# Two operands of an embedding land in pages of the weights' ring, and an empty job stands ahead of the output matrix's last two rows

## The chip, the cores and the metric

The kernel runs on one core of a Trainium2 chip. A core has five engines that matter here, each with a queue of its own that it works off in order: TensorE (PE in the profile; its weight loads are PEld), VectorE (DVE), ScalarE (ACT), GpSimd (POOL) and SyncE (SP), which here only issues DMA transfers. The metric is the device time of one execution in microseconds (us), the median of several runs.

## The reference

The reference is an encoder of two layers over 1024 tokens of width 1024, all in float32. Layer 0 mixes tokens by neighbourhood attention (16 heads of 64, a window of 8 by 16 tokens on a 16 x 64 grid, a learned bias by offset); layer 1 by dense differential attention (8 heads, two softmaxes each). After the mixer each layer has a gated ConvGLU of inner width 2816 and then a gated embedding of the layer's own input `p`:

```python
for i in range(DEPTH):
    h = rms_norm(x, g[0])
    m = neighborhood_attention(...) if i % 2 == 0 else diff_attention(...)
    x = x + rms_norm(m, g[1])
    f = conv_glu_ffn(rms_norm(x, g[2]), ...)
    x = x + rms_norm(f, g[3])
    gate = sigmoid(rms_norm(x, g[4]) @ ple_w_gate[i])
    x = x + gate * (p[i] @ ple_w_proj[i])
```

Two products of this concern the change: `p[i] @ ple_w_proj[i]` (1024 x 256 by 256 x 1024), which depends on no token mixer and so can be computed early, and the attention's own output product with `na_w_o` (`da_w_o` in layer 1), 1024 x 1024.

## The kernel before, in words

**Float32 by three products.** Every operand of a matmul is split into a high part (a rounding copy on ACT, `high`, L135) and a low part (the difference, on DVE, `low`, L138); `mm3` (L172 to L174) multiplies high by high, high by low and low by high. So a page of 128 x 1024 that comes from memory costs one ACT instruction and one DVE instruction before PE can use it.

**Pools.** `raw` has three pages and takes what DMA loads; `ws` has four pages, the ring of the weights: each block of the projection's weights takes two (high and low), and later the embedding's results `e` and the strips of the attention's output take them too. `r1` and `r2` have four pages of 128 x 4096 each; `r1` holds the normed input of the layer, `r2` the queries, keys and values of two pairs of heads. A page is taken again when all who read it are done. All pages of a pool have one size, 4 KB a partition in `raw` and in `ws`.

**The stream.** In `na` (L528) a loop over 64 units (16 heads by 4 pairs of column blocks) computes for unit n+1 the scores and the softmax (`na_scores`), turns unit n's weights (`na_turn`, two groups) and multiplies unit n-2 with its values (`na_values`). In between `tick` draws steps from a generator, `qkv_stream` (L296), so that the projection of the next pair of heads fills PE. At the last pair (j = 7) the stream has four more things at its end: after the first half of the last value projection (L383) it begins `embeddings` (L440), which brings in two blocks of rows of `pT` and two of `ple_w_proj`, splits the four into the pages `a` and `b` of `r2`, and later multiplies them, 8 blocks of tokens by 2 halves, into pages `e` that are written to `pp` (L1476 to L1484); it calls `last_rows` (L707); and it runs `first_out` (L790), the part of the output product that needs only the first seven pairs' results. In layer 0 `embeddings` calls `load_split` four times, each with a page of `raw`; in layer 1 the four are loaded and split one at a time by jobs.

**Jobs.** `last_rows` issues loads of the eight rows of blocks of the output matrix and leaves nine jobs in a list: split rows 0 to 5, then `part` (split the first strip of the attention's output, loaded in row 4's job; it also issues row 7's load), then rows 6 and 7 (row 6's load is issued by row 5's job). One job is drawn at the end of `na_scores` (L471) and one at the end of the second `na_turn` (L492), and its ACT and DVE instructions are ordered behind that step's own on the same engine. In layer 1 `da_scores` (L617) and `da_turn` (L633) draw them in the same way: `last_rows` is shared by both layers. `row` and `first_out` draw jobs themselves where something that they need is not there yet.

**The second strip.** `mix_out` (L803) begins after the loop. Its first act is `second = self.out_part(...)` (L829): a strip of the attention's output is loaded into a page of `raw` and split into two pages of `ws`.

**Order.** PE's instructions stand in the order in which the program is written (L1550). Those of ACT, DVE, POOL and SP are ordered by a planner when the program is built: it takes what is ready by its own account of time, earlier lines of the program first. A wait then holds all that stands behind it in that engine's queue.

Of the kernel before, what the change touches and what calls it, by code (L numbers as in the profile page):

```python
# [91 lines left out]
class Trunk:  # L92
# [27 lines left out]
    def page(self, pool, tag, shape=(P, D), dt=F32, **k):  # L120
        return pool.tile(list(shape), dt, tag=tag, name=self.uid(tag), **k)
# [84 lines left out]
    def bcast(self, pool, tag, row, **k):  # L206
        t = self.page(pool, tag, **k)
        self.nc.sync.dma_start(t, row.partition_broadcast(P))
        return t
# [497 lines left out]
    def last_rows(self, layer):  # L707


        nc = self.nc  # L710
        src = self.i[("na_w_o", "da_w_o")[layer]]
        self.W, self.part0 = [], None
        page = lambda dt=F32R: self.page(self.r1, "r1", (P, 4, D), dt)
        pages = [page(), page(), page(F32)]
        raw = {}

        def load(kt):
            if kt < 4:
                raw[kt] = pages[2][:, kt]
            else:  # L720
                raw[kt] = self.page(self.raw, "raw")
            nc.sync.dma_start(raw[kt], src[kt * P : kt * P + P])

        def row(kt):
            if kt == 4:
                del pages[2]
                pages.extend([page(), page()])
            hi, lo = pages[2 * (kt // 4) : 2 * (kt // 4) + 2]
            parts = hi[:, kt % 4], lo[:, kt % 4]
            did = self.split(raw.pop(kt), *parts)  # L730
            self.W.append(parts)
            if kt == 4:
                raw["part"] = self.part_raw(layer, 0)
            if kt == 5:
                load(6)
            return did

        def part():
            self.part0 = self.part_of(raw.pop("part"))
            load(7)  # L740
            return self.did

        for kt in range(6):
            load(kt)
        self.jobs += [lambda kt=kt: row(kt) for kt in range(6)] + [part] + [lambda kt=kt: row(kt) for kt in (6, 7)]

    def job(self, act, dve):

        if self.jobs:
            self.behind(self.jobs.pop(0)(), (act, dve))  # L750

    def row(self, kt):

        while len(self.W) <= kt:
            self.jobs.pop(0)()
        return self.W[kt]

    def times(self, out, sta, mov, first=True):
# [31 lines left out]
    def first_out(self):  # L790

        while self.part0 is None:
            self.jobs.pop(0)()
        hi, lo = self.part0
        m = [self.bank(self.pj), self.bank(self.pj)]
        yield
        yield from self.times_steps(
            m, [(hi[:, k], lo[:, k]) for k in range(KT - 1)], (self.row(k) for k in range(KT - 1)), last=False
        )
        self.row(KT - 1)  # L800
        self.out0 = hi, lo, m
# [638 lines left out]
    def embeddings(self, layer):  # L1440

        nc = self.nc
        a = self.page(self.r2, "r2", (P, 2, 2, SEQ), F32R)
        b = self.page(self.r2, "r2", (P, 2, 2, D), F32R)
        load = []
        for k in range(2):
            rows = slice(k * P, k * P + P)
            for o, src in ((a, self.i["pT"]), (b, self.i["ple_w_proj"])):
                load.append((src[layer][rows], o[:, k, 0], o[:, k, 1]))
        if layer == 0:  # L1450
            for src, *parts in load:
                self.load_split(src, dst=parts)
        else:
            left = list(load)

            def begin(src, *parts):
                raw = self.page(self.raw, "raw")
                nc.sync.dma_start(raw, src)
                return raw, parts

            next_one = [begin(*left.pop(0))]

            def job():
                raw, parts = next_one.pop()
                did = self.split(raw, *parts)
                if left:
                    next_one.append(begin(*left.pop(0)))
                return did

            self.jobs += [job] * 4  # L1470
        yield
        while layer == 1 and next_one:
            self.jobs.pop(0)()
        for t in range(NT):
            s = slice(t * P, t * P + P)
            e = self.page(self.ws, "ws")  # L1476
            for half in range(2):
                w = slice(half * 512, half * 512 + 512)
                o = self.bank(self.pj)
                for k in range(2):  # L1480
                    self.mm3(o, (a[:, k, 0, s], a[:, k, 1, s]), (b[:, k, 0, w], b[:, k, 1, w]), k == 0, k == 1)
                    yield
                nc.scalar.activation(e[:, w], o, AF.Copy)  # L1483
            nc.sync.dma_start(self.pp[layer][s], e)  # L1484
# [127 lines left out]
```

## Time and profile before

| | |
|---|---|
| Median of 3 runs | 2758.91 us (2757.64 to 2758.96) |
| Profiled execution | 2758.85 us, of which the span from first to last instruction is 2757.1 us |
| Mean granted TensorE clock | 0.993 |
| PE busy | 2693.7 us, 98% of the span |
| PEld, DVE, ACT, POOL busy | 81%, 70%, 48%, 17% |
| DMA in the two stages' ends | the last 60 us of neighbourhood attention are 430 to 490 us; those of differential attention 1850 to 1930 us |

PE's share of busy time is a mean over all stages; what happens at one place is read from the waits, the timeline and the granted clock of that place. The granted clock is 1.00 or 0.50 in stretches of 3.4 us or a multiple of it. "SPq" rows are DMA issues: their time is that of the issue, and the wait for the landing shows in the instruction that needs the data.

### The profile page before, as it was taken

To read this page: it belongs to the slowest core of one execution; us is meant where nothing else is said; L and a number is where in the kernel's file an instruction comes from. 1 tells how busy PE (TensorE), PEld (TensorE's weight loads), DVE (VectorE), ACT (ScalarE), POOL (GpSimd) and SP (SyncE) were. 2 spreads that over 40 slices of the span, in tenths; PEclk is the share of its full clock that TensorE was granted. 3 is DMA by queue.
4 is the path that set the end of the run, shared out by engine and by line. 5 is a ranking of instruction groups with operands and counts; after the bars stand their busy time and mean duration, and the time that the engine had idled before them with its cause. 6 is when DMAs were issued, how large, how long until landed. Compare 5 with 4: busy or idle time off the path is not lost.

```text
span 2757.1 us, 36537 instructions
## 1 busy us (share of the span) xinstructions
PE 2693.7 (98%) x13440; PEld 2225.7 (81%) x13440; DVE 1938.5 (70%) x3317; ACT 1321.2 (48%) x2467; POOL 463.2 (17%) x461
## 2 busy tenths in 40 slices
PE   7999998999999999999999999999999999999998
PEld 5788887877888888888788888887887888888887
DVE  5677776579777777676566666676688777776664
ACT  4555556454444445454355555555454434444452
POOL 2121220004333310001000000000105333300000
PEclk9999999999999999999999999999999999999999
DMA  6512214533322373343211111123413323272342
GB/s 183 169 55 68 66 48 156 142 92 107 115 102 94 115 263 125 105 150 111 99 46 46 45 46 46 53 77 126 134 62 122 115 92 115 98 284 96 115 146 103
DMA packets 129476, 298.48 MB, mean 108 GB/s; under 512 B 11753, under 2 KB 37737, under 8 KB 129297
## 3 DMA queue, kind: packets, MB, share of 16 engines
q1 hardware_dynamic: 129296, 296.15, 32.5%
q8 instruction: 105, 1.72, 0.3%
q14 instruction: 75, 0.61, 0.1%
HBM read 221.69 MB, written 86.61 MB: 112 GB/s over the span
## 4 chain that ended last, share of the span: by engine, by line
PE 85%; DVE 6%; DMA 4%; ACT 2%; issue 2%; POOL 0%; SPq 0%; ACTq 0%; POOLq 0%; DVEq 0%
PE b L172 19%; PE b L173 19%; PE b L174 19%; PE g L770 6%; PE m L770 5%; PE b L642 4%; PE s L606 3%; PE b L628 2%; PE b L203 2%; PE av L512 1%; PE b L485 1%; DVE r L138 1%; PE b L770 1%; DMA raw<-in_qkv 1%; DMA x<-in_x 1%
## 5 line engine op out<-in xcount | busy, mean ns | idle before, releaser
L172 PE MATMUL b<-r,ws 128*128 128x512 f32 (+1 forms) x1328 | 547.3, 412 | 6.9 <-ACT ws L135 3.7
L173 PE MATMUL b<-r,ws 128*128 128x512 f32 (+1 forms) x1328 | 519.7, 391 | 1.4 <-DVE r L138 1.2
L174 PE MATMUL b<-r,ws 128*128 128x512 f32 (+1 forms) x1328 | 519.1, 391 | 0.5 <-DVE ws L138 0.5
L172 PEld LDWEIGHTS b<-r,ws 128*128 128x128 f32 x1328 | 252.8, 190 | 55.2 <-ACT ws L135 4.1
L174 PEld LDWEIGHTS b<-r,ws 128*128 128x128 f32 x1328 | 252.1, 190 | 54.8 <-DVE ws L138 1.0
L173 PEld LDWEIGHTS b<-r,ws 128*128 128x128 f32 x1328 | 253.3, 191 | 38.6 <-DVE r L138 3.5
L172 PE MATMUL b<-r,r 128*128 128x512 f32 x680 | 270.4, 398 | 9.5 <-ACT r L135 5.2
L184 POOL TENSOR_TENSOR ss<-ss,mhalf 128x1 f32<-128x1 f32 x136 | 84.0, 619 | 1142.1 <-DVE ss L646 563.3
L172 PE MATMUL b<-r,wa 128*128 128x512 f32 x688 | 269.0, 391 | 4.5 <-DVE B L1140 3.7
L445 ACT ACTIVATE E<-E,mn 128x1024 f32<-128x1024 f32 (+2 forms) x256 | 221.4, 866 | 105.2 <-DVE mn L441 104.7
L174 PE MATMUL b<-r,wa 128*128 128x512 f32 x688 | 268.6, 390 | 0.0
L173 PE MATMUL b<-r,wa 128*128 128x512 f32 x688 | 268.4, 390 | 0.0
L174 PE MATMUL b<-r,r 128*128 128x512 f32 x680 | 266.5, 392 | 1.0 <-DVE r L138 1.0
L173 PE MATMUL b<-r,r 128*128 128x512 f32 x680 | 266.8, 392 | 0.5 <-DVE r L138 0.5
L138 DVE TENSOR_TENSOR ws<-raw,ws 128x512 fp32r<-128x512 f32 (+3 forms) x168 | 171.1, 1026 | 61.1 <-ACT ws L135 58.6
L138 DVE TENSOR_TENSOR r<-raw,r 128x512 fp32r<-128x512 f32 (+1 forms) x170 | 129.1, 766 | 113.1 <-ACT r L135 110.0
L135 ACT ACTIVATE r<-raw 128x512 fp32r<-128x512 f32 (+1 forms) x170 | 112.7, 670 | 193.2 <-PE b L173 162.6
L135 ACT ACTIVATE ws<-raw 128x512 fp32r<-128x512 f32 (+3 forms) x168 | 124.3, 748 | 137.4 <-PE b L174 52.1
L172 PEld LDWEIGHTS b<-r,r 128*128 128x128 f32 x680 | 128.6, 189 | 38.6 <-ACT ws L1483 6.3
L770 PE MATMUL m<-r,ws 128*128 128x512 f32 x672 | 156.9, 393 | 0.0
L172 PEld LDWEIGHTS b<-r,wa 128*128 128x128 f32 x688 | 129.4, 188 | 33.5 <-DVE B L1140 5.2
L770 PE MATMUL g<-r,ws 128*128 128x512 f32 x672 | 155.8, 391 | 0.0
(178 smaller groups left out, 5110.4 us busy)
## 6 DMA issues: line engine op xcount, KB each, us to landing
raw<-in_w_in SPq DMA_DIRECT2D x86, 512.0 KB, 3.5
raw<-in_qkv SPq DMA_DIRECT2D x48, 512.0 KB, 5.6
spillS<-r SPq DMA_DIRECT2D x88, 256.0 KB, 3.2
r<-in_ffn_w_out SPq DMA_DIRECT2D x40, 512.0 KB, 10.1
raw<-spillS SPq DMA_DIRECT2D x40, 512.0 KB, 3.5
spillA<-B SPq DMA_DIRECT2D x66, 256.0 KB, 2.9
raw<-spillA SPq DMA_DIRECT2D x30, 512.0 KB, 4.0
x<-x SPq DMA_DIRECT2D x24, 512.0 KB, 3.7
```

What stands on the lines that cost most here:

```text
L135: return self.nc.scalar.activation(hi, src, AF.Copy).ins
L138: return self.nc.vector.tensor_tensor(out=lo, in0=src, in1=hi.bitcast(F32), op=ALU.subtract).ins
L172: mm(out, sta[0], mov[0], start=first, stop=False, skip_group_check=onto)
L173: mm(out, sta[0], mov[1], start=False, stop=False, skip_group_check=onto)
L174: mm(out, sta[1], mov[0], start=False, stop=last, skip_group_check=onto)
L184: self.nc.gpsimd.tensor_tensor(out=ss, in0=ss, in1=self.mhalf, op=ALU.pow)
L203: self.nc.tensor.transpose(t[:, k * P : k * P + P], h[:, c : c + P], self.ident)
L445: self.exp = nc.scalar.activation(e, e, AF.Exp, bias=mn, scale=-1.0, accum_out=sm).ins
L606: nc.tensor.matmul(s[m][:, w], A[o, a, q], A[o, b, w], start=z == 0, stop=z == 2)
L628: nc.tensor.transpose(t[:, k * P : k * P + P], w[:, c : c + P], self.ident)
L642: nc.tensor.matmul(o, wT[:, k], V[:, k], start=k == 0, stop=k == KT - 1)
L770: mm(out[half], a, b[:, w], start=first and k + z == 0, stop=last and k == n - 1 and z == 2)
```

## The change

There are two edits. In layer 0's `embeddings` the four pages into which DMA loads are taken first, in the order `raw`, `ws`, `ws`, `raw`, and then each operand is loaded and split: the second and the third (the first block of `ple_w_proj`, the second of `pT`) land in pages of `ws`. In `last_rows` the list of jobs gets an entry `None` after `part`: the step that draws it has nothing to add, and rows 6 and 7 are drawn one step later, in both layers. The places that draw a job are taught to skip an empty one (`hurry`, and a test in `job`).

```diff
-        self.jobs += [lambda kt=kt: row(kt) for kt in range(6)] + [part] + [lambda kt=kt: row(kt) for kt in (6, 7)]
+        self.jobs += [lambda kt=kt: row(kt) for kt in range(6)] + [part, None] + [lambda kt=kt: row(kt) for kt in (6, 7)]

     def job(self, act, dve):

         if self.jobs:
-            self.behind(self.jobs.pop(0)(), (act, dve))
+            todo = self.jobs.pop(0)
+            if todo:
+                self.behind(todo(), (act, dve))
+
+    def hurry(self):
+
+        todo = self.jobs.pop(0)
+        if todo:
+            todo()

     def row(self, kt):

         while len(self.W) <= kt:
-            self.jobs.pop(0)()
+            self.hurry()
         return self.W[kt]
...
         if layer == 0:
-            for src, *parts in load:
-                self.load_split(src, dst=parts)
+            raws = [self.page(p, t) for p, t in ((self.raw, "raw"), (self.ws, "ws"), (self.ws, "ws"), (self.raw, "raw"))]
+            for raw, (src, *parts) in zip(raws, load):
+                nc.sync.dma_start(raw, src)
+                self.split(raw, *parts)
```

`first_out` and the wait loop of layer 1's `embeddings` call `hurry` in the same way.

More of the change, by code (lines that the diff above doesn't have):

```diff
@@ L792, in first_out @@
         while self.part0 is None:
-            self.jobs.pop(0)()
+            self.hurry()
         hi, lo = self.part0
@@ L1472, in embeddings @@
         while layer == 1 and next_one:
-            self.jobs.pop(0)()
+            self.hurry()
         for t in range(NT):
```

## The prediction

> **What bounds the kernel now.** I read the page first, for the span and the chain that ended last; then PE's waits around the end of neighbourhood attention; then that stretch by windows, with the granted clock; then the timelines of SP, ACT and DVE there.
>
> ```profile
> span 2757.1 us, 36537 instructions
> PE 85%; DVE 6%; DMA 4%; ACT 2%; issue 2%; POOL 0%; SPq 0%; ACTq 0%; POOLq 0%; DVEq 0%
> ```
>
> PE sets the time nearly everywhere; a gain can come only where PE waits, or from the clock that it is granted behind a wait. In 430 to 500 us, the end of neighbourhood attention, these are PE's longest waits (total, times, longest):
>
> ```profile
> PE b L172 <- ACT r L135: 5.2, 1, 5.2
> PE b L172 <- ACT ws L1483: 3.3, 1, 3.3
> PE b L770 <- ACT ws L1483: 1.3, 1, 1.3
> ```
>
> Windows of that stretch (length; busy time and count of PE, PEld, DVE, ACT, POOL; granted clock; DMA share, GB/s) show that the two long waits each cost twice: PE is then granted half of its clock for 6.8 us.
>
> ```profile
> 433.30:440.10 6.80, 1.79 (x11) 1.25 (x9) 3.44 (x7) 3.04 (x7) 0.00 (x0) 1.00 0.98 360
> 440.10:447.00 6.90, 5.71 (x15) 4.32 (x16) 3.44 (x10) 3.45 (x8) 0.00 (x0) 0.51 0.25 85
> 470.80:477.70 6.90, 6.25 (x17) 5.29 (x18) 3.00 (x9) 3.30 (x9) 0.00 (x0) 0.51 0.57 178
> ```
>
> The chain that ended last names what the waits hang on (start, length): a load of the embedding for the first, a row of the output matrix for the second, a store of `pp` for the third.
>
> ```profile
> 431.90 7.79 DMA raw<-in_ple_w_proj
> 464.26 5.57 DMA raw<-in_na_w_o
> 478.80 3.09 DMA pp<-ws
> ```
>
> **The change, part by part. First, the embedding's operands.** No instruction is added: four loads, four ACT copies and four DVE differences stay. Only the pages, and so the times of the loads, move. SP's issues before:
>
> ```profile
> 390.42 0.38 SPq L161 DMA_DIRECT2D raw<-in_pT  x1
> 402.38 0.33 SPq L161 DMA_DIRECT2D raw<-in_ple_w_proj  x1
> 427.50 1.75 SPq L722 DMA_DIRECT2D r<-in_na_w_o  x4
> 429.37 0.60 SPq L161 DMA_DIRECT2D raw<-in_pT  x1
> ```
>
> The first two take the free pages of `raw`; the last two wait until the first two are split, and then queue behind four rows of the output matrix: the fourth lands 7.79 us after 431.90. In the changed kernel the fourth operand takes the page of 402.38, and the second and third need two pages of `ws`. The last weights of queries leave theirs when PE has read them, at 415:
>
> ```profile
> 414.94 0.39 PE L174 MATMUL b<-r,ws 128*128 128x512 f32 x1
> 415.20:426.50 11.30, 11.30 (x63) 9.75 (x62) 7.29 (x22) 6.28 (x16) 0.00 (x0) 1.00 0.01 1
> ```
>
> There DMA is idle (share 0.01), and SP issues nothing between 402.38 and 427.50, so nobody stands behind these two as they wait for PE. Even at the jam's 7.79 us they land by 423, before the first split could run:
>
> ```profile
> 426.52 1.05 ACT L135 ACTIVATE r<-raw 128x1024 fp32r<-128x1024 f32 x1
> 434.77 0.60 ACT L135 ACTIVATE r<-b 128x512 fp32r<-128x512 f32 x1 [0.47 <-PE b L203]
> 439.71 1.06 ACT L135 ACTIVATE r<-raw 128x1024 fp32r<-128x1024 f32 x1 [1.49 <-DMA raw<-in_ple_w_proj]
> 440.80 1.23 DVE L138 TENSOR_TENSOR r<-raw,r 128x1024 fp32r<-128x1024 f32 x1 [1.32 <-ACT r L135]
> 442.08 0.79 PE L173 MATMUL b<-r,r 128*128 128x512 f32 x1 [0.47 <-DVE r L138]
> 427.60:435.40 7.80, 7.14 (x42) 5.84 (x40) 6.56 (x14) 5.28 (x11) 0.00 (x0) 1.00 0.89 288
> ```
>
> The late splits then move from the stall (439.71 on ACT is the later) in among the work of the last unit but five. That cover is thin: from 427.6 to 435.4 DVE is busy 6.56 of 7.80 us, and two more differences are 2 x 1.23 = 2.46, so 6.56 + 2.46 - 7.80 = 1.2 us do not fit and reach PE through the softmax and the evacuations. If instead the planner leaves both splits where they stand now, behind the last evacuation of values (ACT free at 435.3), they end at about 435.3 + 1.05 + 1.23 + 1.23 = 438.8. PE's two waits of 5.2 + 0.47 = 5.7 us so shrink by 5.7 - 1.2 = 4.5 at best and by 442.1 - 438.8 = 3.3 at worst. I take 4.2, near the best, because the planner takes earlier lines first and the splits' lines are early.
>
> The clock: 5.71 us of PE at 0.51 did the work of 2.9, so 2.8 us were lost. Smaller waits can cost a stretch too:
>
> ```profile
> 638.10:641.50 3.40, 1.22 (x6) 0.77 (x5) 3.40 (x5) 1.95 (x4) 2.10 (x2) 1.00 0.52 190
> 641.50:644.90 3.40, 3.40 (x10) 2.62 (x9) 3.40 (x6) 0.00 (x0) 0.86 (x2) 0.50 0.67 211
> ```
>
> Here PE was busy 1.22 of 3.4 us (its one wait is 2.18) and got half the clock for the next 3.4: 1.7 us. With a wait of 1.4 to 2 PE is busy over 40% of such a stretch and I take no loss; the bound is 1.7. **First term: 4.2 + 2.8 = 7.0 us; bounds 3.3 + 1.1 = 4.4, and 5.7 + 2.8 = 8.5.**
>
> [...]
>
> **Second, the empty job in layer 0.**
>
> ```profile
> 467.38 0.84 ACT L135 ACTIVATE Ahi<-b 128x512 fp32r<-128x512 f32 x2
> 469.85 1.06 ACT L135 ACTIVATE r<-raw 128x1024 fp32r<-128x1024 f32 x1 [1.63 <-DMA raw<-in_na_w_o]
> 470.82 1.06 ACT L1483 ACTIVATE ws<-b 128x512 f32<-128x512 f32 x2
> ```
>
> Row 6's copy waits 1.63 us for its load and runs 1.0; behind it stand two evacuations that PE waits for. One step later (behind the next exponentials) its load, landed at 469.83, is there. The evacuation then starts at 468.2 instead of 470.82, and PE's wait of 3.3 falls to about 0.6: 2.7 us. The clock stretch after it goes: 6.25 us at 0.51, 3.1 us. Row 7 moves from where row 6 then stands to behind the following turn; its load, issued when the first strip is split, has some 6 us, against 5.57 for row 6's.
>
> What is late next is the second strip, whose load takes the page that row 6 leaves:
>
> ```profile
> 472.33 0.38 SPq L779 DMA_DIRECT2D raw<-oT  x1
> 477.19 1.05 ACT L135 ACTIVATE r<-raw 128x1024 fp32r<-128x1024 f32 x1
> DMA to landing us min/median/max: 4.1/4.3/4.4
> 481.99 0.95 ACT L135 ACTIVATE ws<-raw 128x896 fp32r<-128x896 f32 x1 [1.11 <-DMA pp<-ws]
> 483.59 0.60 ACT L1483 ACTIVATE ws<-b 128x512 f32<-128x512 f32 x1
> ```
>
> Today that strip's copy (481.99) waits for a store, and the last evacuation of the embedding stands behind it; PE waits 1.3 for that one until 483.59 + 0.60 = 484.2. In the same frame of time (the first term left out) PE, 2.7 + 3.1 = 5.8 us ahead, ends the embedding at 484.2 - 1.3 - 5.8 = 477.1. Row 6 is copied where row 7 is today (477.19), some 4.5 earlier, as 1.3 of the clock's gain lies behind that place: 472.7, and its page is free at 472.7 + 1.05 + 1.2 = 474.9, so the strip lands at 474.9 + 4.4 = 479.3. The planner ranks the strip's copy below the evacuation and runs it first only if it believes it ready first; it now lands 2 us after the evacuation is due, so I take the evacuation first: PE goes on at 477.9, a gain of 484.2 - 477.9 = 6.3 for all three waits and the clock. If the strip keeps its place: 479.3 + 0.95 + 0.6 + 0.6 = 481.5, a gain of 2.7, less 3.4 for 6.8 us at half clock after a wait of 4.3: -0.7. **Second term: 6.3; bounds -0.7 and 3.3 + 3.1 + 1.3 = 7.7.**
>
> **Third, the empty job in layer 1,** which shares the list.
>
> ```profile
> 1892.32 1.15 ACT L445 ACTIVATE E<-E,mn 128x1024 f32<-128x1024 f32 x1 [1.08 <-DVE mn L441]
> 1894.37 1.06 ACT L135 ACTIVATE r<-raw 128x1024 fp32r<-128x1024 f32 x1 [0.33 <-DMA raw<-in_da_w_o]
> 1896.47 1.04 ACT L135 ACTIVATE r<-raw 128x1024 fp32r<-128x1024 f32 x1
> 1902.89 0.95 ACT L135 ACTIVATE ws<-raw 128x896 fp32r<-128x896 f32 x1 [3.81 <-DMA pp<-ws]
> 1904.22 1.14 ACT L445 ACTIVATE E<-E,mn 128x1024 f32<-128x1024 f32 x1
> 1904.38 0.47 PE L628 MATMUL b<-ident,E 128*128 128x128 f32 x1 [3.27 <-ACT wT L631]
> 1904.40:1907.80 3.40, 3.40 (x10) 2.71 (x11) 1.33 (x5) 3.23 (x7) 0.00 (x0) 0.50 0.30 124
> ```
>
> Rows 7 and 6 are copied at 1894.37 and 1896.47, ahead of the evacuations whose store the strip's copy awaits; PE stands 3.27 us behind that, and then 3.4 us at half clock (1.7). With the empty job row 6 takes the earlier step (behind the turn, where ACT idles 1.08 ahead of 1892.32) and row 7 an iteration later. The evacuations and the store come forward by 1.0 to 2.1 us, one or both copies. I take 1.5 and keep the half clock, since a wait of 1.8 is left. **Third term: 1.5; bounds 3.27 + 1.7 = 5.0, and -2, two displaced copies in front of PE.**
>
> Sum: 7.0 + 6.3 + 1.5 = 14.8. The profiled execution took 2758.85 us, of which 2757.1 is the span; its time is 0.06 under the median of the runs. 2758.85 - 14.8 = **2744.0 us**.
>
> **The rivals.** *A, the strip keeps its place* in layer 0: its copy stays ahead of the last evacuation and a wait of some 4 us stands where 3.3 + 1.3 stood. For it: the planner has put it there now, and put row 6 ahead of evacuations though its load came 1.63 late. Against: the load moves back and the evacuation forward. 7.0 - 0.7 + 1.5 = 7.8: 2751.0 us.
>
> *B, the splits stay late:* the loads are early but the planner keeps the two copies behind the values' evacuation. For it: DVE has 1.2 us free there, and the first split, loaded at 390.42, did not run before 426.52. First term 4.4, sum 12.2: 2746.7 us.
>
> *C, slower: the strip takes row 7's page in both layers* and its copy keeps its place. Row 7 is displaced furthest. In layer 0 the strip then lands some 2.4 later, at 481.7, and PE goes on at 484.5: a third wait of 7 us eats what the second and its clock gave (-0.3), and 6.8 us at half clock follow it: -0.3 - 3.4 = -3.7. In layer 1 row 7 moves behind the exponentials of the next iteration, 8.6 us on (1904.22 - 1892.32, less the wait of 3.27), and the strip and PE's restart with it: -8.6 + 2.1 = -6.5, and 1.7 of clock: -8.2. Sum 7.0 - 3.7 - 8.2 = -4.9: 2763.8 us. It decides where the strip lands after 1900.9 with the turned weights' copy behind it. Against: row 6's page is free first.
>
> *D, nothing comes forward:* the planner gives the pages of 415 to no load before the jam, and the second term is lost to A. For it: a page of `ws` is asked for by the embedding's results too, but those are written from 443 on. 2758.9 us.
>
> [...]
>
> **How the numbers follow.** Forecast 0.46, A 0.19, B 0.13, C 0.06, D 0.09, E 0.07. About 0.2%, 5.5 us, is what a measurement can tell from no change. Faster: forecast, B, E and most of A, 0.80; within 0.2%: D and the rest of A, 0.13; slower: C and a little of D, 0.07. The forecast's own range is 2740 to 2748.5; for 8 in 10 it reaches down to all three terms near their best (8.5 + 7.7 + 4 = 20: 2739) and up past A to 2754.5.
>
> **What would show it.** Right: loads of `in_pT` and `in_ple_w_proj` into `ws` at about 415; no wait of 5.2 at L172; clock 1.00 from 440 to 447 and from 464 on; L1483 straight after the turn's copies; PE's restart after the embedding within 1 us. Wrong: a half clock stretch in either place; the strip's copy ahead of the last L1483 with PE idle over 3 us; in layer 1 a wait at L628 of 3.27 or more; or lost time in stages that the change does not touch, since the planner orders all anew.

## The result, and the profile after

The changed kernel takes 2742.42 us (median of 4 runs, 2741.7 to 2744.52), the kernel before, on the same chip, 2758.93 (4 runs, 2757.64 to 2760.32): a ratio of 0.9940, with a 95% interval of 0.9928 to 0.9952. Predicted were 2744.0 us. The profiled execution took 2742.31 us. One run of the kernel with one page, below, took 7112 us at a granted clock of 0.507 and is left out of that kernel's median. The head of the changed kernel's page, span and shares of the chain that ended last:

```profile
span 2740.5 us, 36536 instructions
PE 86%; DVE 6%; DMA 3%; ACT 2%; issue 2%; POOL 0%; SPq 0%; ACTq 0%; POOLq 0%; DVEq 0%
```

TensorE's instructions stand in the same order in both kernels, so its k-th matmul of the one can be set against the k-th of the other. These are the steps of that shift over five stretches, in us (minus is a gain); they are worked out from the two traces, and for the kernels of the experiments below in the same way. A wait belongs to the stretch in which it ends, and "all" is the shift of the last matmul. "Head" is all up to 141 us, "first" 432.6 to 454.1 us of the kernel before, "second" 467.8 to 499.8, "third" 1887 to 1917.7, and "rest" what lies between and behind these.

```
kernel                                  head   first  second  third   rest    all
changed, first profile                  -1.4    -5.8    -6.3   -3.4   +0.4  -16.5
changed, second profile                 +1.1    -7.3    -6.3   -3.3   +0.8  -15.1
predicted                                 0     -7.0    -6.3   -1.5     0   -14.8
pages only                              -1.2    -5.8    -1.7   -0.7   -1.5  -10.9
empty job only                          +0.6    +0.2    -6.4   -3.3   -0.7   -9.6
empty job in layer 0 only               -3.4    -7.3    -6.4   +0.1   -1.0  -18.0
differences on GpSimd                   +0.6    -4.7    -6.3   -3.4   -0.1  -13.8
fourth operand later                    +0.3    -7.4    -6.3   -1.5   +0.1  -14.8
no differences                          -0.1    -8.2    -6.3   -3.1   -1.5  -19.2
one page                                +0.7    -5.3    -6.3   -3.4   -0.4  -14.7
```

"Head" and "rest" hold nothing that the change touches; between profiles they differ by up to 4.5 and 2.3 us. So the three middle columns are where to look, and the sum of a single profile is good to a few us only.

**In layer 0** these are TensorE's waits in 420 to 490 us of the changed kernel (total, times, longest). The waits of 5.2, 3.3 and 1.3 us are gone; a new one of 1.7 stands at L485. L1493 and L778 are L1483 and L770 of the kernel before.

```profile
PE b L485 <- DVE sum L469: 1.7, 1, 1.7
PE b L172 <- ACT ws L1493: 0.6, 1, 0.6
PE b L778 <- ACT ws L1493: 0.5, 1, 0.5
PE b L203 <- DVE Alo L138: 0.3, 1, 0.3
```

Windows of the same stretch (length; busy time and count of PE, PEld, DVE, ACT, POOL; granted clock; DMA share, GB/s): half a clock is left only behind the new wait, for 3.4 us, and the stretch behind the second wait runs at full clock.

```profile
431.84:435.25 3.41, 1.60 (x10) 1.30 (x11) 3.04 (x8) 1.84 (x4) 0.00 (x0) 1.00 1.03 371
435.25:438.67 3.42, 3.42 (x12) 3.03 (x11) 1.60 (x5) 0.98 (x3) 0.00 (x0) 0.50 0.58 228
...
463.90:470.80 6.90, 6.45 (x36) 5.19 (x34) 5.98 (x13) 6.50 (x13) 0.00 (x0) 1.00 0.69 235
```

The timeline of SP shows the loads (start, length): the two into `ws` go out as soon as the weights' pages are free, 12 us ahead of the rows of the output matrix. The two into `raw` (at 414.61 and 415.13, left out) stand behind them in SP's queue and so are later than the 390 and 402 us of before, which costs nothing: their first copy on ACT runs at 425.14.

```profile
413.75 0.33 SPq L1461 DMA_DIRECT2D ws<-in_ple_w_proj  x1
414.13 0.42 SPq L1461 DMA_DIRECT2D ws<-in_pT  x1
...
426.12 1.75 SPq L722 DMA_DIRECT2D r<-in_na_w_o  x4
```

What makes the new wait is seen in the timelines of PE and DVE. L485 needs a bank that DVE frees with the difference `r<-b` (432.51 to 433.20); that one stands behind the embedding's last difference (430.54, 1.22 us) and L522, left out here. The view names the reciprocal L469 instead, which ends on DVE at about the same time (433.33); in the kernel with the fourth operand later, below, it names `r L138`.

```profile
433.34 0.41 PE L485 MATMUL b<-ident,E 128*128 128x128 f32 x2 [1.72 <-DVE sum L469]
```

```profile
430.54 1.22 DVE L138 TENSOR_TENSOR r<-raw,r 128x1024 fp32r<-128x1024 f32 x1
...
432.51 0.69 DVE L138 TENSOR_TENSOR r<-b,r 128x512 fp32r<-128x512 f32 x1
```

At the end of the embedding ACT's timeline shows rows 6 and 7 copied without a wait (465.62 and 467.78, the second left out), the last evacuation at 470.13, and the second strip's copy behind it, late by 0.81 us with nobody of TensorE's behind it:

```profile
465.62 1.04 ACT L135 ACTIVATE r<-raw 128x1024 fp32r<-128x1024 f32 x1
470.13 0.60 ACT L1493 ACTIVATE ws<-b 128x512 f32<-128x512 f32 x1
471.97 0.95 ACT L135 ACTIVATE ws<-raw 128x896 fp32r<-128x896 f32 x1 [0.81 <-DMA raw<-oT]
```

**In layer 1** the strip's copy (1887.47) keeps its place ahead of the turned weights' copy L631, but it waits 2.26 us where it waited 3.81: rows 6 (1878.26) and 7 (1891.54, left out) both lie outside the evacuations whose store it awaits. PE's wait at L628 falls from 3.27 to 0.7 us, and the window behind it has the full clock. ACT's timeline, PE's waits and the window:

```profile
1878.26 1.05 ACT L135 ACTIVATE r<-raw 128x1024 fp32r<-128x1024 f32 x1
1887.47 0.95 ACT L135 ACTIVATE ws<-raw 128x896 fp32r<-128x896 f32 x1 [2.26 <-DMA pp<-ws]
1888.33 0.58 ACT L631 ACTIVATE wT<-b 128x512 f32<-128x512 f32 x1
```

```profile
PE b L628 <- ACT wT L631: 0.7, 1, 0.7
PE b L778 <- ACT ws L1493: 0.6, 1, 0.6
```

```profile
1888.90:1892.30 3.40, 2.73 (x14) 2.13 (x15) 1.25 (x5) 3.40 (x7) 0.00 (x0) 1.00 0.28 114
```

### The profile page after: what moved, and what is told of

It reads as the page before. It is cut to its first block, busy times and chain, and to the rows that moved or that the text cites. A ratio compares the mean times of both kernels' runs of the same rounds, so it can differ in the third digit from the quotient of the medians.

```text
span 2740.5 us, 36536 instructions
## 1 busy us (share of the span) xinstructions
PE 2685.8 (98%) x13440; PEld 2220.6 (81%) x13440; DVE 1939.2 (71%) x3317; ACT 1319.9 (48%) x2467; POOL 463.8 (17%) x461
## 3 DMA queue, kind: packets, MB, share of 16 engines
q8 instruction: 105, 1.72, 0.3%
## 4 chain that ended last, share of the span: by engine, by line
PE 86%; DVE 6%; DMA 3%; ACT 2%; issue 2%; POOL 0%; SPq 0%; ACTq 0%; POOLq 0%; DVEq 0%
PE b L172 20%; PE b L173 20%; PE b L174 19%; PE g L778 6%; PE m L778 5%; PE b L642 4%; PE s L606 3%; PE b L628 2%; PE b L203 2%; PE av L512 1%; PE b L485 1%; DVE r L138 1%; DMA raw<-in_qkv 1%; PE b L778 1%; DMA x<-in_x 1%
## 5 line engine op out<-in xcount | busy, mean ns | idle before, releaser
L138 DVE TENSOR_TENSOR ws<-raw,ws 128x512 fp32r<-128x512 f32 (+3 forms) x168 | 172.2, 1032 | 59.6 <-ACT ws L135 56.5
L138 DVE TENSOR_TENSOR r<-raw,r 128x512 fp32r<-128x512 f32 (+1 forms) x168 | 126.9, 762 | 106.7 <-ACT r L135 103.5
L778 PE MATMUL m<-r,ws 128*128 128x512 f32 x672 | 156.0, 391 | 0.0
L778 PE MATMUL g<-r,ws 128*128 128x512 f32 x672 | 155.8, 391 | 0.0
L441 DVE CUSTOM_DVE_ANT_0 E<-s,T 128x1024 f32<-128x1024 f32 x128 | 151.1, 1218 | 3.6 <-PE s L606 3.6
```

The costliest lines, as they stand in the source:

```text
L138: return self.nc.vector.tensor_tensor(out=lo, in0=src, in1=hi.bitcast(F32), op=ALU.subtract).ins
L441: nc.vector.tensor_tensor_reduce(out=e, in0=s, in1=bias, scale=1.0, scalar=3e38, op0=ALU.add, op1=ALU.min, accum_out=mn)
L778: mm(out[half], a, b[:, w], start=first and k + z == 0, stop=last and k == n - 1 and z == 2)
```

## The experiments

All diffs are against the changed kernel. Four ran beside each other with the kernel before at 2757.64 us (11 runs, 2755.30 to 2760.73), the other four with it at 2758.82 (11 runs, 2755.73 to 2762.58).

**The pages alone.** No empty job.

```diff
-        ... + [part, None] + [lambda kt=kt: row(kt) for kt in (6, 7)]
+        ... + [part] + [lambda kt=kt: row(kt) for kt in (6, 7)]
```

> The embedding's pages alone; the list of jobs is as before. Theory (each edit takes away a wait of its own): PE's wait of 5.2 us at the embedding is gone and a wait of about 1.7 for DVE stands ahead of it, some 5.6 us less; the wait of 3.3 behind row 6 and its 6.8 us at half clock stay, and layer 1's wait of 3.3 stays: about 2753.3 us. Rival 1 (the earlier loads free the queue, so that row 6 lands in time by itself, and the empty job is idle): as the changed kernel, 2742.4 us. Rival 2 (the planner's new order elsewhere, not these waits, made the gain): no wait removed here shows in the time, or time moves in other stages.

Measured: 2749.19 us (7 runs, 2747.97 to 2752.46), ratio 0.9970 (0.9959 to 0.9982). PE's waits in 415 to 500 us, then in layer 1, and the windows around the second wait:

```profile
PE b L172 <- ACT ws L1493: 2.9, 1, 2.9
PE b L485 <- DVE sum L469: 1.7, 1, 1.7
...
PE b L628 <- ACT wT L631: 1.9, 1, 1.9
```

```profile
462.24:465.65 3.41, 1.50 (x7) 1.29 (x8) 1.55 (x2) 2.03 (x3) 0.00 (x0) 1.00 0.58 209
465.65:469.06 3.41, 3.41 (x11) 2.92 (x10) 1.66 (x8) 2.10 (x6) 0.00 (x0) 0.50 0.88 259
```

The first term is there whole (-5.8, as in the first profile of the changed kernel, with the same wait of 1.7). The gain, 8.5 us against the kernel before beside it, is more than the 5.6 that the expectation put down to the pages; the profile is that of the fastest of the seven runs. The second wait stayed, at 2.9, but was followed by 3.4 us at half clock where the kernel before has 6.8 (-1.7 in that column, 0.3 of it from the wait). The wait at L628 was 1.9 where it was 3.3, and a wait of 0.6 at L778 is new (-0.7 together). ACT's copies stand there in the order of the kernel before; the store that the strip's copy awaits let it go 3.5 us after its issue (1889.33 to 1892.87) and not 4.6 (1898.27 to 1902.89). Why it landed sooner was not taken apart.

**The empty job alone.** The embedding's operands as in the kernel before.

```diff
-            raws = [self.page(p, t) for p, t in (...)]
-            for raw, (src, *parts) in zip(raws, load):
-                nc.sync.dma_start(raw, src)
-                self.split(raw, *parts)
+            for src, *parts in load:
+                self.load_split(src, dst=parts)
```

> The empty job alone, in both layers; the embedding's four operands land in raw as before. Theory: the wait of 5.2 us at 430 to 441 and its half clock stay; behind it the wait of 3.3 shrinks to about 0.6 with no half clock (6.4 us), and layer 1's wait of 3.3 shrinks to under 1 (some 3.4 us with the clock): 2758.9 - 9.8 = about 2749.1 us. Rival 1 (the empty job is idle once the loads are early, and here it only moves the wait to the second strip): 2758.9 us or within 2 of it.

Measured: 2749.33 us (5 runs, 2745.54 to 2750.55), ratio 0.9964 (0.9951 to 0.9976), against 2749.1 expected. PE's first wait stays; in layer 1 the wait at L628 is short:

```profile
PE b L172 <- ACT r L135: 5.7, 1, 5.7
...
PE b L628 <- ACT wT L631: 0.8, 1, 0.8
```

The 9.8 us of the expectation are 9.6 in the profile and 8.3 between the medians. The two edits do not need each other: alone they bring 8.5 and 8.3 us (each against 2757.64), 16.8 together, and the changed kernel brings 16.5.

**The empty job in layer 0 only.**

```diff
-        ... + [part, None] + ...
+        ... + [part] + [None] * (layer == 0) + ...
```

> Both edits, but the empty job in layer 0 alone. Theory: layer 1's wait of 3.3 at the turned weights comes back, 2.5 us more, and with it the 3.4 us at half clock behind it (1.7): 2742.4 + 4.2 = about 2746.6 us. Rival (the shift seen in layer 1 was the clock's chance, not the job's): 2742.4 to 2744 us, with the wait of 3.3 gone all the same or costing no clock.

Measured: 2745.35 us (5 runs, 2740.90 to 2746.04), ratio 0.9950 (0.9937 to 0.9962): the spread of the runs does not tell it from the changed kernel. The profile, of the fastest of these runs, does. In layer 1 PE's wait and the half clock behind it are back, and the third column of the table is +0.1:

```profile
PE b L628 <- ACT wT L631: 2.6, 1, 2.6
```

```profile
1885.03:1888.44 3.41, 1.11 (x7) 0.79 (x7) 1.82 (x3) 3.21 (x6) 0.00 (x0) 1.00 0.27 81
1888.44:1891.86 3.42, 3.42 (x10) 2.77 (x11) 2.35 (x5) 1.53 (x4) 0.00 (x0) 0.50 0.37 153
```

Against this kernel the empty job is worth 3.5 us in layer 1; against the pages alone, which have no empty job there either, it is 2.7. In layer 0 this kernel has the same wait of 1.7 at L485 and no half clock behind it; the last section takes that up.

**The embedding's four differences on GpSimd**, to free VectorE where the new wait arises.

```diff
-                self.split(raw, *parts)
+                self.high(raw, parts[0])
+                nc.gpsimd.tensor_tensor(out=parts[1], in0=raw, in1=parts[0].bitcast(F32), op=ALU.subtract)
```

> Both edits, and the four differences of the embedding's operands in layer 0 (4 x 1.23 us on DVE) are taken by POOL, which is idle from 415 to 485. Theory (the 1.7 us wait at 433 is DVE's crowd, and the half clock behind it follows from PE busy under half of 3.4 us): the wait falls to about 0.5 and the clock stays at 1.00: 2742.4 - 1.2 - 1.7 = about 2739.5 us. Rival 1 (the wait is ACT's, whose four copies stay): within 1 us of 2742.4. [...]

Measured: 2743.61 us (5 runs, 2742.50 to 2744.62), ratio 0.9947 (0.9934 to 0.9959). The wait at L485 is gone, but one of 3.46 us stands a little behind it, and the gain of the first stage is the smallest of all kernels with the pages, 4.7. The timelines of POOL, DVE and PE show why (in brackets the idle time ahead, and what ended it):

```profile
421.93 2.39 POOL L1463 TENSOR_TENSOR r<-ws,r 128x1024 fp32r<-128x1024 f32 x1 [6.73 <-ACT r L135]
...
434.03 2.45 POOL L1463 TENSOR_TENSOR r<-raw,r 128x1024 fp32r<-128x1024 f32 x1
```

```profile
422.68 1.86 DVE L470 TENSOR_SCALAR E<-E,sum 128x384 f32<-128x384 f32 x1
...
426.79 0.42 DVE L470 TENSOR_SCALAR E<-E,sum 128x384 f32<-128x384 f32 x1
...
433.54 0.75 DVE L470 TENSOR_SCALAR E<-E,sum 128x384 f32<-128x384 f32 x1
...
434.39 2.31 DVE L470 TENSOR_SCALAR E<-E,sum 128x384 f32<-128x384 f32 x1
```

```profile
437.45 1.09 PE L203 MATMUL b<-ident,raw 128*128 128x128 f32 x4 [3.46 <-DVE Alo L138]
```

L470 takes 0.42 us alone. Beside a difference on GpSimd it takes 1.86, 0.75 and 2.31, and each time ends 0.22 or 0.23 us after that difference (424.54 against 424.32, 434.29 against 434.06, 436.70 against 436.48; the one that ends at 434.06 is left out). So moving the work did not free VectorE; it held up the softmax, and behind it `Alo`, which PE waits for at L203. The time is neither the theory's 2739.5 nor within 1 us of 2742.4, as rival 1 had it.

**The fourth operand later:** its split is ordered behind that of the turned values (the one that frees L485's bank).

```diff
             for raw, (src, *parts) in zip(raws, load):
                 nc.sync.dma_start(raw, src)
-                self.split(raw, *parts)
+                raw is raws[3] or self.split(raw, *parts); self.fourth = lambda: self.behind(self.split(raws[3], *load[3][1:]), self.last)
...
                 def put(g, t):
-                    self.split(t, o[:, :, :, 0:64], o[:, :, :, 64:128])
+                    self.last = self.split(t, o[:, :, :, 0:64], o[:, :, :, 64:128])
...
-                        self.transposed(vT, put, groups=(0,))
+                        self.transposed(vT, put, groups=(0,)); layer or j < KT - 1 or self.fourth()
```

> As the changed kernel, but the embedding's fourth operand is split behind the split of the turned values (the one that frees the bank that L485 waits for at 433.34 us) instead of ahead of it; nothing else moves by more than a place. Theory (VectorE is full there, so 1.2 us of its work reach TensorE wherever the difference stands): the wait of 1.7 us at L485 shrinks to about 0.5, and the 1.2 us come back at the next instruction that VectorE releases (L203 or L512, behind Alo); the time stays within 1.5 us of the changed kernel's 2742.4. Rival (only the order is bad): the wait goes without another in its place, and with it the half clock behind it: 1.2 to 1.7 us and 1.7 us less, 2739 to 2741 us.

Measured: 2743.0 us (5 runs, 2741.68 to 2744.09), ratio 0.9942 (0.9930 to 0.9954). PE's waits:

```profile
PE b L203 <- DVE sum L469: 1.4, 1, 1.4
PE b L485 <- DVE r L138: 0.6, 1, 0.6
```

The theory held: 1.7 + 0.3 became 0.6 + 1.4, the same 2.0 us at another place. The order is not what costs.

**No differences.** The four low parts in layer 0 are left out and the high parts are multiplied in their place, so layer 0's embedding comes out about three times as large; PE's matmuls are the same in number and shape.

```diff
-                self.split(raw, *parts)
+                self.high(raw, parts[0])
...
-    self.mm3(o, (a[:, k, 0, s], a[:, k, 1, s]), (b[:, k, 0, w], b[:, k, 1, w]), k == 0, k == 1)
+    self.mm3(o, (a[:, k, 0, s], a[:, k, layer, s]), (b[:, k, 0, w], b[:, k, layer, w]), k == 0, k == 1)
```

> As the changed kernel, but the four low parts of the embedding's operands in layer 0 are left out: no differences on VectorE, and the high parts stand in for them in the products (so layer 0's embedding is less exact; TensorE has as many matmuls as before). This takes 4 x 1.22 us from VectorE. Theory (the rest of the first wait is VectorE's work that did not fit): no wait above 0.7 us from 425 to 447 us and no half clock there; the shift against the kernel before grows from 5.6 us to 9 us in that stage, the time is 2739 us. Rival (the bank or ScalarE, not VectorE, sets the wait): the wait of 1.7 us stays, 2742.4 us.

Measured: 2740.61 us (5 runs, 2739.37 to 2741.69), ratio 0.9933 (0.9921 to 0.9944). The wait at L485 is gone, but not all of the rest:

```profile
PE b L203 <- DVE Alo L138: 1.2, 1, 1.2
```

Of 2.0 us of waiting 0.8 went with 4.9 us of VectorE's work, and the stage is 0.9 better than in the second profile of the changed kernel, which has no half clock there either. Both sides were wrong in part: VectorE's differences are 0.8 us of it, not all and not nothing. The rest is ScalarE's by this trace. ACT is busy without a gap from 428.60 to 434.29, with two of the embedding's copies first; the copy `Ahi` that `Alo` reads ends there at 433.53, and DVE begins `Alo` 0.11 us later:

```profile
432.95 0.58 ACT L135 ACTIVATE Ahi<-b 128x512 fp32r<-128x512 f32 x1
```

```profile
433.64 1.11 DVE L138 TENSOR_TENSOR Alo<-b,Ahi 128x512 fp32r<-128x512 f32 x2
```

No run moved those copies, so this share is read and not tested. The kernel before waits 0.6 at L203 too.

**One page** of `ws` and not two.

```diff
-            ... ((self.raw, "raw"), (self.ws, "ws"), (self.ws, "ws"), (self.raw, "raw"))]
+            ... ((self.raw, "raw"), (self.ws, "ws"), (self.raw, "raw"), (self.raw, "raw"))]
```

> As the changed kernel, but only the second operand lands in a page of ws (order raw, ws, raw, raw). Theory (the fourth load waits until the first operand is split and then queues behind four rows of the output matrix, as in the kernel before): the wait for the fourth operand is back, 3.5 to 5 us and 3.4 to 6.8 us at half clock, without the wait of 1.7 at L485: a loss of 3.5 to 6 us against the changed kernel, 2746 to 2748.5 us. Rival (one page is enough): 2742.4 us.

Measured: 2744.1 us (5 runs, 2742.85 to 2745.95), ratio 0.9946 (0.9933 to 0.9959). PE's waits in 415 to 500 us, and the load that is late on SP:

```profile
PE b L485 <- DVE sum L469: 1.7, 1, 1.7
PE b L173 <- DVE r L138: 0.8, 1, 0.8
PE b L172 <- ACT r L135: 0.7, 1, 0.7
```

```profile
430.06 0.39 SPq L1461 DMA_DIRECT2D raw<-in_ple_w_proj  x1
```

The fourth load does wait for the first split and does queue behind four rows of the output matrix, as the theory said. But it goes out at 430.06, not at 431.90 as the last one of the kernel before, and only one split is late. By ACT's copy of it (437.31, without idle time ahead) it has landed. PE waits 0.8 + 0.7 for that copy and its difference, not 3.5 to 5, so the loss that was expected did not come. The second page is worth 2.0 us by the profiles (5.3 against 7.3, both without half clock) and too little for the times: 2744.1 against 2743.25.

**The changed kernel once more,** as a measure of what profiles differ by.

> The changed kernel once more, beside the others, as a measure of what a profile differs by without any change: median 2742.4 us, within 1.5. If half clock behind waits of 1.5 to 2.3 us is chance, the stretches at 435, 641, 1929 and 2074 us will not all be as in the first profile of it; if it is set by the kernel, they will be.

Measured: 2743.25 us (5 runs, 2740.26 to 2743.87), ratio 0.9940 (0.9928 to 0.9952). All waits of the two ends are as in the first profile; the half clock is not. Windows, on the 3.41 us grid in which the clock changes, and the wait at L485 from PE's timeline:

```profile
431.80:435.21 3.41, 2.27 (x12) 1.52 (x11) 3.35 (x8) 3.36 (x9) 0.00 (x0) 1.00 0.93 354
435.21:438.63 3.42, 2.53 (x15) 2.10 (x16) 2.83 (x8) 0.99 (x3) 0.00 (x0) 1.00 0.97 367
...
1909.76:1913.18 3.42, 1.48 (x12) 1.25 (x11) 0.56 (x2) 0.67 (x3) 0.55 (x1) 1.00 0.35 117
1913.18:1916.59 3.41, 3.41 (x9) 2.66 (x9) 1.24 (x2) 2.38 (x7) 0.00 (x0) 0.50 0.47 190
```

```profile
435.79 0.41 PE L485 MATMUL b<-ident,E 128*128 128x128 f32 x2 [1.72 <-DVE sum L469]
```

The same wait of 1.72 us ends here at 435.79, 2.4 us later than in the first profile, because the kernel's start took longer. It so falls across two windows, of which PE is busy 2.27 and 2.53 us, and none is followed by half clock; in the first profile it fell into one (busy 1.60), and 1.7 us were lost. At 1909.76 it is the other way round: half here, full in the first profile. No kernel that computes the whole beats the changed one by more than such chances.

## Why the prediction was right, point by point

**What bounds the kernel.** Right: only PE's waits and the clock behind them moved, and nothing that the change does not touch moved by more than the profiles of one kernel differ by.

**First term, 7.0: right in its mechanism and, without the clock's chance, in its size.** The two loads into `ws` are where they were forecast, at 414 us. That "nobody stands behind these two" in SP's queue was wrong: the embedding's own two loads into `raw` do, at no cost. The waits of 5.2, 0.6 and 0.5 in the kernel before (the second is the row below, of its PE timeline) became 1.7 and 0.3: 4.3 us, where 4.2 were taken. The 2.8 of clock came back too, as the second profile and the kernel with the empty job in layer 0 only show (7.3 in both). The step that failed in the first profile is "with a wait of 1.4 to 2 PE is busy over 40% of such a stretch and I take no loss; the bound is 1.7". PE was busy 47% of that window and the bound came true. A half clock stretch in this place is also one of the prediction's own signs of being wrong; it showed in one profile of two. The 1.2 us of VectorE "that do not fit" were a good guess at the size of the new wait (2.0, less the 0.6 that stood at L203 before), and half right as its cause: 0.8 by the kernel without the differences, and the rest ScalarE's, as far as that trace tells.

```profile
434.08 0.66 PE L203 MATMUL b<-ident,raw 128*128 128x128 f32 x4 [0.57 <-DVE sum L469]
```

**Second term, 6.3: right in size and in its steps.** 6.3 in both profiles of the changed kernel, and between 6.3 and 6.4 in every kernel that has the empty job in layer 0. The restart after the embedding takes 0.5 us, and the planner did put the last evacuation ahead of the strip's copy. Rival A falls with that row, and C with the wait of 0.7 in layer 1.

**Third term, 1.5: the mechanism was right, the size was not.** It measured 3.4. The step was "I take 1.5 and keep the half clock, since a wait of 1.8 is left". Both row copies left the place ahead of the strip, so the wait fell by 2.5 us and 0.7 was left. The half clock then went, and gave about 0.9 more: 1.7, less a wait of 0.6 at L778 that now shows and smaller losses that were not taken apart. The kernel with the fourth operand later shows how near this is to the edge: the wait at L628 is 1.0, the window is busy 1.75 of 3.41 us, half clock follows, and its third step is 1.5.

```profile
1887.85:1891.26 3.41, 1.75 (x10) 1.17 (x9) 1.46 (x3) 3.41 (x6) 0.00 (x0) 1.00 0.01 2
1891.26:1894.67 3.41, 3.41 (x13) 2.95 (x12) 2.81 (x6) 2.02 (x5) 0.00 (x0) 0.50 0.37 154
```

**The other rivals.** B, splits that stay late, is out: the last difference runs at 430.54. D is out by the times. E stood for 2742.3 us, without half clock behind layer 1's remaining wait: nearest of all to the measured 2742.4. The clock there was 1.00 in the first profile of the changed kernel (window of 1888.90), but behind a wait of 0.7 and not of the forecast's 1.8; and half clock followed windows in which PE was busy for 1.60 us (changed kernel, layer 0) and 1.75 us (fourth operand later, layer 1).

**The sum.** 14.8 were forecast. The first profile has 15.5 in the three terms and 1.0 at the start and elsewhere, where nothing was changed; the second has 16.9 and loses 1.9 there. The medians differ by 16.5 (first set of runs) and 15.6 (second). That the sum came so near the first profile's 15.5 is in part luck: the first term was 1.2 too large for it and the third 1.9 too small.

## What to carry to other kernels

When two late operands hold up an engine, look for a page of another ring that is free before the jam; here the second page mattered less than the first (5.3 of 7.3 us came with one), because one late load among the jam was nearly on time. An entry that only delays a list of side jobs by one step can be worth as much as an earlier load (8.3 and 8.5 us here), where a copy that waits for its load stands in a queue ahead of copies that TensorE waits for. Price a wait together with the window of the clock in which it will fall (here one wait of 1.72 us lost 1.7 us of clock in one profile and none in the other), and before reading a difference of 2 us from a single profile take another of the same kernel.

## What the runs showed of the hardware that was not expected

**Half clock followed windows in which TensorE had worked for up to 1.75 us.** For windows of 3.41 us at full clock (the grid on which the clock changes in these profiles) these are PE's busy times in us, by the clock that the next window was granted:

```
kernel                     next at 0.50                    next at 1.00
before                     0.00, 0.15, 0.76, 1.22, 1.48    1.81, 1.85
changed, first profile     1.15, 1.60                      1.94, 2.11
changed, second profile    1.17, 1.48                      2.03, 2.27
pages only                 1.02, 1.50                      1.51
empty job only             0.00                            1.69
empty job in layer 0 only  1.11                            1.64
differences on GpSimd      0.64
fourth operand later       1.21, 1.75                      2.01, 2.13
one page                                                   1.68
```

From 1.50 to 1.75 us both are seen, three times half and four times full. The kernel with the pages alone has both within 0.01 us: 1.50 and then half clock (shown above), and 1.51 and then full:

```profile
1916.30:1919.71 3.41, 1.51 (x7) 1.30 (x8) 0.56 (x2) 1.05 (x4) 0.55 (x1) 1.00 0.68 229
1919.71:1923.12 3.41, 3.41 (x16) 2.82 (x16) 1.86 (x4) 2.08 (x6) 0.55 (x1) 1.00 0.28 102
```

The wait of 1.72 us at L485 cost 1.7 us more in the first profile of the changed kernel, where it fell inside one window (busy 1.60), and nothing more in the second, where it fell across two (2.27 and 2.53). At four places with waits of 1.7 to 2.3 us (433, 627, 1911 and 2073 us of the changed kernel) this can move a single profile by up to 4 x 1.7 = 6.8 us, by estimate; each of its two profiles paid at two of them.

**Beside GpSimd's differences one VectorE operation took longer and three did not.** L470 took 1.86, 0.75 and 2.31 us for 0.42, while L441, L522 and the difference `r<-b` ran beside them at 0.55, 0.69 and 0.69 (0.55, 0.68 and 0.69 in the changed kernel). What sets L470 apart was not tested.
